# Retention with the last 16 keys as the left-over group, and other PSUM banks for the second feed-forward's first sums

## The chip, the cores and the metric

The kernel runs on one core of one Trainium2 chip. The metric is the device time of one execution in microseconds (us); less is better. Before the change it is 1469.22 us, the median of three runs (1469.2 to 1470.43).

## The reference

One block works on T = 528 tokens, 16 learned meta tokens followed by 512 real ones, of width 1024: a gated feed-forward, a mixer and a second gated feed-forward, each with a norm ahead and a residual sum behind it. The mixer projects its input to queries, keys, values and gates of two branches, retention and sparse attention, adds the two gated results and projects the sum. The part that matters here is retention, with 4 heads, keys of 256 and values of 512. The reference writes it chunk by chunk with a state:

```
inner = (q k^T * d_in) v            # within a chunk of 128 tokens
cross = (q state) * xi              # everything before the chunk
state = g_chunk * state + (k * zeta)^T v
y = concat(y_meta, inner + cross);  y = y / rms(y);  out = (silu(rg) * y) @ w_ret_out
```

Unrolled, the output of token i is the sum over all tokens j up to i of (q_i . k_j) times a power of the head's decay (the power is i - j) times v_j. The kernel computes it in that form. The meta tokens come first and every real token sees them. All numbers are fp32. The result holds the 512 real tokens.

## The kernel before

TensorE gets each fp32 operand as a high and a low part, and each product is three matmuls (high x high, high x low, low x high). The splits are a copy on ACT (the high part) and a subtraction on DVE or GpSimd (the low part), at lines 325 and 326 for most operands. Products go to PSUM. In the mixer four single banks (tag `sm`, taken in turn) and two double banks (tag `mm`) serve all products; a tile from a tag can be written once the tile that held that bank has been read.

The program is written out in one order (a manual schedule): each engine runs its instructions in the order in which the code issues them, and semaphores make it wait for others. The mixer is a list of steps, one for each tile of a projection's weights. Work of retention is hung into these steps.

For each head h:

- `fetch_head` and `new_decay` load values, gates and the table of decay powers from DRAM by SP's queue. `place_tails` (GpSimd's queue) puts the left-over values, the 16 meta tokens' in `vtail`, in three row groups (high, high, low).
- `values_in` (lines 1732 and 1735) splits the values.
- `decayed` (lines 1776 to 1800) makes five groups of score matmuls, six matmuls each. Groups `kb` = 0 to 3 hold 128 real keys, from token 16 + 128 kb on, against the 512 - 128 kb queries that can see them. The fifth holds the 16 meta keys against all 512 queries. Each product `psst` is multiplied by the decay on DVE into a scratch tile (`tmp`, four in turn) and split (`ph`, `pl`; `ptail` for the fifth).
- `weigh` (lines 1810 to 1821) multiplies the weights with the values, 128 queries at a time. One last matmul takes all left-over keys with its three products stacked in its rows (`ptail`, `vtail`). ACT squares the result for the norm, DVE multiplies it with the gate.

For head 0 this lies beside projections (`psgate`, `psrq`). For heads 1 to 3 it lies in `outputs(h-1)`, the four steps of the output projection of the head before. Each step makes two tiles `psro` in the `sm` banks, which ACT copies out (line 1955 into `accr`, or 1958 into `RR` for GpSimd to add). Behind the two tiles of step 1 come `values_in`, of step 2 `decayed`, of step 3 `weigh`. The gates' Silu (line 1745) is issued between the two tiles of step 2.

Values reach DRAM after their projection: the 512 real tokens' as `vrs`, the 16 meta tokens' by `last_tokens` (line 1400), which computes them in a small product behind the others and splits them, as `vd`.

The second feed-forward begins where the mixer's output tiles `psmo` end (line 158). `enter` (line 2690) closes the mixer's PSUM pools and opens `f2ps` for its first sums, `psd` (line 2653). The tags `d0` and `d1` come first in it. DVE adds each `psmo` tile to the residual (`hc`, line 2746).

Of the kernel before, what the change touches and what calls it, by code (L numbers as in the profile page):

```python
# [47 lines left out]

UW = NM + S


def _constants():

    pos = np.arange(T, dtype=np.float32)
    rope = np.zeros((3, 2, P, T), np.float32)
    for i, d in enumerate((64, 128, 256)):
        expo = -np.arange(0, d, 2, dtype=np.float32) / np.float32(d)
        freq = (10000.0 ** expo.astype(np.float64)).astype(np.float32)
        ang = (freq[:, None] * pos[None, :]).astype(np.float64)
        reps = P // (d // 2)  # L60
        cos = np.tile(np.cos(ang), (reps, 1))
        sin = np.tile(np.sin(ang), (reps, 1))
        if d < 256:
            sign = np.where((np.arange(P) % d) < d // 2, -1.0, 1.0)
            sin = sin * sign[:, None]
        rope[i, 0] = cos.astype(np.float32)
        rope[i, 1] = sin.astype(np.float32)
    decay = np.zeros((RH, P, UW), np.float32)
    diff = np.arange(UW)[None, :] - np.arange(P)[:, None]
    for h in range(RH):  # L70
        lg = math.log1p(-(2.0 ** (-5.0 - h)))
        decay[h] = np.where(diff >= 0, np.exp(lg * np.maximum(diff, 0)) * DK**-0.5, 0.0)
    causal = np.zeros((P, S), np.float32)
    p = np.arange(P)
    causal[:, S - P :] = np.where(p[None, :] <= p[:, None], 0.0, NEG)
    return {"rope": rope, "decay": decay, "causal": causal}
# [3 lines left out]
def kernel(ctx: ExitStack, tc: tile.TileContext, x, meta, g1, wg1, wu1, wd1, gm,  # L80
# [216 lines left out]
    vst = dpool.tile([2, P, 4, 4, P], F32, name="vst")  # L297
    vrs_d = dpool.tile([RH, P, 4, S], F32, name="vrs")
    rgs = dpool.tile([RH, 2, P, 2 * S], F32, name="rgs")
# [409 lines left out]
    if True:  # L709
# [574 lines left out]

        ret_k, ret_q = [], []
        tables = []

        def bring():
            hall_r = fp.tile([P, 4352], F32R, tag="hT", name="rqk")
            for at, c0, width, n in ((ret_k, 0, 576, T), (ret_q, 2304, S, S)):  # L1290
                off = width - n
                at.extend(tuple(hall_r[:, c0 + (2 * j + i) * width + off :][:, :n] for j in range(2)) for i in range(2))
            for i in range(2):
# [32 lines left out]
        class Values:  # L1326
# [36 lines left out]
            def leave(self, i, half, r):  # L1363
# [4 lines left out]
                elif self.kind == "values":  # L1368
                    nc.gpsimd.dma_start(vrs_d[i, :, 2 * half : 2 * half + 2, :].rearrange("p b c -> p (b c)"), r)
                else:  # L1370
                    nc.gpsimd.dma_start(rgs[i, half], r)
# [15 lines left out]
            def last_tokens(self):  # L1387
# [3 lines left out]
                for i, qs in enumerate((("11", "12"), ("21", "22"))):  # L1391
                    for k in range(KD):
                        for c in range(4):
                            nc.tensor.matmul(ps[32 * c : 32 * c + 32, i * P : (i + 1) * P], dv["last"][:, k, :],
                                             self.q[qs[k // 4]][:, k % 4, c * P : (c + 1) * P],
                                             start=k == 0, stop=k == KD - 1)
                r = room("rest")[:, : 4 * P]
                split(ps[:, : 2 * P], r[:, : 2 * P].bitcast(F32R), r[:, 2 * P :].bitcast(F32R))
                for i in range(2):
# [245 lines left out]
    if True:  # L1645
# [13 lines left out]
        def bring_more():  # L1659

            new_decay(0)
            fetch_head(0)
            place_tails(0)
            nc.gpsimd.dma_start(ka[:64, :S], fs[:64, 0, :])
# [40 lines left out]
        def new_decay(h):  # L1705
            u = heads[h]["u"] = rt.tile([P, UW], F32, tag="u", name="u")
            nc.sync.dma_start(u, decay[h])

# [3 lines left out]
        def fetch_head(h):  # L1712
# [3 lines left out]
            else:  # L1716
                v = vraw().rearrange("p (b c) -> p b c", b=4)
                vparts["l"] = [v[:, :2], v[:, 2:]]
            for i, v in enumerate(vparts["l"]):
                nc.sync.dma_start(v, vrs_d[h, :, 2 * i : 2 * i + 2])  # L1720
            heads[h]["g"] = [room4("g") for _ in range(2)]
# [6 lines left out]
        def values_in(h):  # L1728
# [4 lines left out]
            def low(i):  # L1733
                eng = nc.gpsimd if h else nc.vector
                eng.tensor_tensor(lo[i].bitcast(F32R), lo[i], hi[:, 2 * i : 2 * i + 2].bitcast(F32), ALU.subtract)
            low(0)
            if h:
                low(1)
            else:
                heads[0]["low"] = low  # L1740
# [35 lines left out]
        def decayed(h):  # L1776
            rq, rk, u = ret_q, ret_k, heads[h]["u"]
            prob, low = [], lambda: None
            for kb in range(5):
                kn, n, q0 = (P, S - kb * P, kb * P) if kb < 4 else (NM, S, 0)  # L1780
                ps = sm_tile("psst")
                ks = slice(NM + kb * P, NM + (kb + 1) * P) if kb < 4 else slice(0, NM)
                for k in range(2):
                    for i, (a, b) in enumerate(((rk[k][0], rq[k][0]), (rk[k][0], rq[k][1]), (rk[k][1], rq[k][0]))):
                        nc.tensor.matmul(ps[:kn, :n], a[:, ks], b[:, q0:],
                                         start=k == 0 and i == 0, stop=k == 1 and i == 2)
                t = tmp()
                u0 = 0 if kb < 4 else NM
                TT(t[:kn, :n], ps[:kn, :n], u[:kn, u0 : u0 + n], ALU.mult)
                low()  # L1790
                if kb < 4:
                    ph = rt.tile([P, n], F32R, tag=f"ph{kb}", name="ph")
                    pl = rt.tile([P, n], F32R, tag=f"pl{kb}", name="pl")
                    low = in_two(t[:, :n], ph, pl)
                    prob.append((ph, pl))
                else:
                    split_rows(t[:NM, :n], tp["p"], "hlh")
            heads[h]["prob"] = prob

        def weigh(h, b):  # L1800
# [5 lines left out]
            for kb in range(b + 1):  # L1806
                ph, pl = (p[:, (b - kb) * P : (b - kb + 1) * P] for p in d["prob"][kb])
                hi, lo = vh[:, kb, :], vl[kb // 2][:, kb % 2, :]
                for i, (a, v) in enumerate(((ph, hi), (ph, lo), (pl, hi))):
                    nc.tensor.matmul(ps, a, v, start=kb == 0 and i == 0, stop=False)  # L1810
            nc.tensor.matmul(ps, tp["p"][:TR, qs], tp["v"][:TR, :], start=False, stop=True)
            if b == 0:
                d["sum"] = rt.tile([P, 8], F32, tag="osum", name="osum", bufs=2)
            nc.scalar.activation(RR[:, 2 * S : 3 * S], ps, AF.Square, accum_out=d["sum"][:, b : b + 1])
            g = d["g"][b // 2][:, b % 2]
# [180 lines left out]
        def trip(h, between=None):  # L1996
# [4 lines left out]
            if h + 1 < RH:  # L2001
                place_tails(h + 1)

# [89 lines left out]
        tp.update(pool=rt, bufs=4)  # L2093
        tails(rt)
        ia, ib = (rt.tile([P, 4, S], F32, tag=f"o{c}", name="ixs") for c in "hl")
# [594 lines left out]
    def enter():  # L2690
# [4 lines left out]
        mixps.close()  # L2695
        f2["ps"] = ctx.enter_context(pool("f2ps", 1, PSUM))
        f2["rooms"] = ctx.enter_context(pool("rooms2", 1))
        f2["later"] = ExitStack()
# [357 lines left out]
```

## Time and profile before

| what | value |
|---|---|
| median of three runs | 1469.22 us (1469.2 to 1470.43) |
| the profiled execution, device time | 1468.84 us |
| its span, first to last instruction | 1467.1 us |
| TensorE busy | 1458.2 us, 99% of the span |
| VectorE (DVE) busy | 1151.5 us, 78% |
| ScalarE (ACT) busy | 781.4 us, 53% |
| GpSimd (POOL) busy | 288.8 us, 20% |
| mean granted TensorE clock | 0.999 |

The span is 1.7 us shorter than the device time of the same run. Busy shares are means over the whole span. An instruction's row in a timeline has its start, its duration, engine, line, operation, what it writes and reads with partitions x elements, how many like it follow each other (xN), and in brackets the idle time of its engine before it and what ended that. Durations of matmuls overlap: the distance of their starts tells what each costs.

### The profile page before, as it was taken

Reading aid. Unit: us, or ns where it says so; the run is one execution under the profiler, and the core shown is the slowest. Engines: PE = TensorE matmul, PEld = TensorE weight load, DVE = VectorE, ACT = ScalarE, POOL = GpSimd, SP = SyncE. Lnnn points to the kernel's source line nnn. Section 1 sums busy time; section 2 is a strip of 40 time slices with the busy share of each in tenths; the row PEclk is TensorE's granted clock in tenths of the full one; section 3 lists DMA queues with packets and bytes.
Section 4 is the critical chain, followed back from the end, with each engine's and each line's share of the span. In section 5 each row is a group of like instructions: output and inputs, shape, how many; then the busy total and the mean of one; then the engine's idle time right before and its main releaser. Section 6 shows DMA issues by size and latency. Waiting matters only on the chain.

```text
span 1467.1 us, 22451 instructions
## 1 busy us (share of the span) xinstructions
PE 1458.2 (99%) x8626; PEld 1286.1 (88%) x8626; DVE 1151.5 (78%) x1688; ACT 781.4 (53%) x1117; POOL 288.8 (20%) x354
## 2 busy tenths in 40 slices
PE   9999999999999999999999999999999999999998
PEld 8999999999988888888888889988888888888887
DVE  5998888876787986588788898888557787767776
ACT  6656455454354554567454547877534644434444
POOL 1101111002100001232152342444103211211110
PEclk9999999999999999999999999999999999999999
DMA  5458787556734554465336443676656476466323
GB/s 175 102 158 202 183 186 192 134 140 196 250 133 160 169 172 151 153 206 173 118 129 211 144 147 101 193 201 204 207 181 213 154 227 202 133 199 207 122 80 122
DMA packets 209563, 246.79 MB, mean 168 GB/s; under 512 B 31568, under 2 KB 153160, under 8 KB 209456
## 3 DMA queue, kind: packets, MB, share of 16 engines
q1 hardware_dynamic: 171504, 179.74, 38.6%
q0 software_dynamic: 34032, 58.78, 16.4%
q10 hardware_dynamic: 3920, 6.84, 1.4%
q8 instruction: 68, 1.11, 0.3%
q14 instruction: 39, 0.32, 0.1%
HBM read 205.52 MB, written 39.60 MB: 167 GB/s over the span
## 4 chain that ended last, share of the span: by engine, by line
PE 95%; DVE 2%; DMA 1%; ACT 1%; issue 0%; POOL 0%; ACTq 0%; DVEq 0%; POOLq 0%
PE psd L2781 8%; PE psvX L1431 7%; PE psqX L2616 7%; PE psqX L158 7%; PE psro L158 6%; PE psqZ L158 5%; PE psd L158 4%; PE psqY L2616 4%; PE psvY L1431 4%; PE psak L158 3%; PE psaq L158 3%; PE psga L158 3%; PE psat L158 3%; PE psmo L158 3%; PE psdX L158 2%; PE psrk L158 2%
## 5 line engine op out<-in xcount | busy, mean ns | idle before, releaser
L326 DVE TENSOR_TENSOR wlo<-raw,whi 128x1024 fp32r<-128x1024 f32 (+2 forms) x138 | 155.2, 1126 | 41.9 <-ACT whi L325 41.2
L325 ACT ACTIVATE whi<-raw 128x1024 fp32r<-128x1024 f32 (+2 forms) x138 | 130.0, 943 | 87.2 <-PE psat L158 9.4
L326 DVE TENSOR_TENSOR wlo<-w,whi 128x1024 fp32r<-128x1024 f32 x96 | 116.8, 1218 | 61.9 <-ACT whi L325 61.8
L325 ACT ACTIVATE whi<-w 128x1024 fp32r<-128x1024 f32 x96 | 101.6, 1058 | 103.7 <-PE psd L2781 39.3
L158 PE MATMUL psro<-o,whi 128*128 128x512 f32 x256 | 79.0, 390 | 0.0
L325 ACT ACTIVATE whi<-wsum 128x1024 fp32r<-128x1024 f32 (+1 forms) x48 | 48.3, 1006 | 36.9 <-PE psdY L158 10.3
L115 ACT ACTIVATE whi<-raw 128x1024 fp32r<-128x1024 f32 (+1 forms) x43 | 43.7, 1016 | 35.3 <-PE psat L158 12.2
L116 DVE TENSOR_TENSOR wlo<-raw,whi 128x1024 fp32r<-128x1024 f32 (+1 forms) x43 | 52.7, 1228 | 9.2 <-ACT whi L115 9.2
L2579 POOL DMA_DIRECT2D hts<-cross x40 | 26.0, 658 | 166.0 <-DVE cross L2576 166.0
L158 PEld LDWEIGHTS psro<-o,whi 128*128 128x128 f32 x256 | 47.9, 188 | 10.3
L2781 PE MATMUL psd<-wlo,hh 128*128 128x512 f32 (+1 forms) x148 | 56.7, 383 | 0.0
L2781 PE MATMUL psd<-whi,hl 128*128 128x512 f32 (+1 forms) x148 | 56.7, 383 | 0.0
L2781 PE MATMUL psd<-whi,hh 128*128 128x512 f32 (+1 forms) x148 | 56.7, 383 | 0.0
L326 DVE TENSOR_TENSOR wlo<-wsum,whi 128x1024 fp32r<-128x1024 f32 (+1 forms) x48 | 55.1, 1152 | 1.2 <-ACT whi L325 0.8
L1959 POOL TENSOR_TENSOR accr<-accr,RR 128x512 f32<-128x512 f32 x24 | 37.3, 1558 | 65.7 <-ACT RR L1958 65.7
L158 PE MATMUL psro<-o,wlo 128*128 128x512 f32 x128 | 49.8, 389 | 0.0
L1431 PE MATMUL psvX<-wlo,th 128*128 128x512 f32 x120 | 46.8, 390 | 0.0
L1431 PE MATMUL psvX<-whi,th 128*128 128x512 f32 x120 | 46.7, 389 | 0.0
L1431 PE MATMUL psvX<-whi,tl 128*128 128x512 f32 x120 | 46.7, 389 | 0.0
L158 PE MATMUL psqX<-xh,whi 128*128 128x264 f32 x144 | 40.8, 283 | 0.0
L158 PE MATMUL psqZ<-xh,wlo 128*128 128x264 f32 x144 | 40.8, 283 | 0.0
L158 PE MATMUL psqX<-xh,wlo 128*128 128x264 f32 x144 | 40.8, 283 | 0.0
(622 smaller groups left out, 5024.8 us busy)
## 6 DMA issues: line engine op xcount, KB each, us to landing
w<-in_w_in_dram SPq DMA_DIRECT2D x40, 512.0 KB, 4.6
raw<-in_w_in_dram SPq DMA_DIRECT2D x27, 512.0 KB, 4.2
raw<-in_w_in_dram SPq DMA_DIRECT2D x13, 1024.0 KB, 6.1
raw<-in_ffn_w_down_dram SPq DMA_DIRECT2D x24, 512.0 KB, 4.2
raw<-in_ffn_w_up_dram SPq DMA_DIRECT2D x11, 1024.0 KB, 5.1
raw<-in_ffn_w_gate_dram SPq DMA_DIRECT2D x10, 1024.0 KB, 5.2
ws<-in_ffn_w_up_dram POOLq DMA_DIRECT2D x20, 512.0 KB, 5.9
w<-in_ffn_w_up_dram SPq DMA_DIRECT2D x20, 512.0 KB, 5.0
```

The source lines that it names most:

```text
L115: nc.scalar.activation(hi, src, AF.Copy)
L116: eng.tensor_tensor(lo, src, hi.bitcast(F32), ALU.subtract)
L158: nc.tensor.matmul(o, a[:, k, :], b[:, sl], start=first and k == 0 and i == 0, stop=last and k == nk - 1 and i == 2, skip_group_check=onto)
L325: nc.scalar.activation(hi, src, AF.Copy)
L326: return lambda: nc.vector.tensor_tensor(lo, src, hi.bitcast(F32), ALU.subtract)
L1431: nc.tensor.matmul(d[bank_][t], a, b[:, k, :], start=not onto and j + k + m == 0, stop=j + k == 3 and m == 2, skip_group_check=onto)
L1959: nc.gpsimd.tensor_tensor(a, a, t, ALU.add)
L2579: nc.gpsimd.dma_start(d.rearrange("(b i) a e -> a i b e", i=32)[a], cross[32 * a : 32 * a + 32].rearrange("p b c t -> p b (c t)"))
L2616: nc.tensor.matmul(ps[:, t], a, b[:, k, :], start=not onto and j + k + m == 0, stop=j + k == 3 and m == 2, skip_group_check=onto)
L2781: nc.tensor.matmul(ps, a, m[:, j, cs], start=first and i == 0, stop=last and i == 2)
```

## The change

Tiles of keys now begin with the meta tokens: the four score groups hold tokens 0 to 127, 128 to 255 and so on of the 528. Queries stay cut at 16 + 128 b. The tile b of queries therefore sees the tiles of keys 0 to b, and what is left over for it are its own last 16 tokens as keys, which only the same 16 see as queries. The left-over keys of all four tiles are taken together in one group: 64 keys (4 x 16) against 64 queries (4 x 16), of which the four 16 x 16 blocks on the diagonal are used. The group has a decay table of its own, 64 x 64, with zeros off these blocks.

- The keys of the fifth group are not contiguous in SBUF; ACT copies them to a scratch tile in two copies (`last_k`, of 48 and 16 columns in four parts).
- `ptail` gets the diagonal blocks in 32-row pieces: four ACT copies and two DVE subtractions, each 32x2x16, instead of two and one of 16x512. The last matmul has 96 rows instead of 80.
- `vtail` holds the left-over values of two tiles side by side. `place_last` loads them unsplit by four DMAs of GpSimd's queue, and `split_last`, called in `values_in`, splits them by two ACT copies and one DVE subtraction of 32x1024. Before, split rows were loaded.
- The values are loaded by four DMAs instead of two, and the decay by two instead of one; `vrs` is laid out by rows of tokens. `last_tokens` copies the values by ACT without a split and sends half as many DMAs for them.
- The decay table takes the part of `RR` where the squares were written; the squares go to another part or to `caus`.
- In `enter`, two tiles with the tags `z` and `x` are taken first, so `d0` and `d1` lie in other banks.

```diff
-                    nc.gpsimd.dma_start(vrs_d[i, :, 2 * half : 2 * half + 2, :].rearrange("p b c -> p (b c)"), r)
+                    nc.gpsimd.dma_start(vrs_d[i, half * 2 * P : (half + 1) * 2 * P].rearrange("(b p) c -> p b c", p=P),
+                                        r.rearrange("p (b c) -> p b c", b=2))
...
+                if self.kind == "values":
+                    nc.scalar.activation(r[:, : 2 * P], ps[:, : 2 * P], AF.Copy)
+                    nc.gpsimd.dma_start(vd[2 * self.u : 2 * self.u + 2, 0].rearrange("i p d -> p i d"),
+                                        r[:, : 2 * P].rearrange("p (i d) -> p i d", i=2))
+                    return
...
+    TK = 3 * 2 * NM
+
+    def retention_tails(p):
+
+        t = p.tile([P, S], F32R, tag="ptail", name="ptail")
+        nc.gpsimd.memset(t[:TK].bitcast(F32), 0.0)
+        tp.update(v=p.tile([P, 2, S], F32R, tag="vtail", name="vtail"), p=t)
+
+    def place_last(h):
+
+        rows = vrs_d[h].rearrange("(b p) c -> b p c", p=P)
+        for b in range(4):
+            r = 4 * NM + b % 2 * NM
+            nc.gpsimd.dma_start(tp["v"][r : r + NM, b // 2].bitcast(F32), rows[b, P - NM :])
+
+    def split_last():
+
+        t, n = tp["v"], 2 * NM
+        for i in range(2):
+            nc.scalar.activation(t[i * n : (i + 1) * n], t[2 * n : 3 * n].bitcast(F32), AF.Copy)
+        return lambda: nc.vector.tensor_tensor(t[2 * n : 3 * n], t[2 * n : 3 * n].bitcast(F32), t[:n].bitcast(F32), ALU.subtract)
...
-            u = heads[h]["u"] = rt.tile([P, UW], F32, tag="u", name="u")
-            nc.sync.dma_start(u, decay[h])
+            u = heads[h]["u"] = RR[:, 2 * S : 3 * S], rt.tile([NT, NT + 16], F32, tag="ulast", name="ulast")[:, :NT]
+            nc.sync.dma_start(u[0], decay[h, :, NM:UW])
+            nc.sync.dma_start(u[1], decay[h, :NT, UW:])
...
-            for i, v in enumerate(vparts["l"]):
-                nc.sync.dma_start(v, vrs_d[h, :, 2 * i : 2 * i + 2])
+            a, b = vparts["l"]
+            rows = vrs_d[h, P - NM : S - NM].rearrange("(b p) c -> b p c", p=P)
+            nc.sync.dma_start(a[NM:, 0], vrs_d[h, : P - NM])
+            nc.sync.dma_start(a[:NM, 0].rearrange("q (c d) -> q c d", c=4), vd[h, 0].rearrange("(c q) d -> q c d", q=32)[:NM])
+            nc.sync.dma_start(a[:, 1], rows[0])
+            nc.sync.dma_start(b, rows[1:].rearrange("b p c -> p b c"))
...
+            last = split_last()
             low(0)
+            last()
...
-            for kb in range(5):
-                kn, n, q0 = (P, S - kb * P, kb * P) if kb < 4 else (NM, S, 0)
-                ps = sm_tile("psst")
-                ks = slice(NM + kb * P, NM + (kb + 1) * P) if kb < 4 else slice(0, NM)
+            def scored(ps, keys, queries):
                 for k in range(2):
-                    for i, (a, b) in enumerate(((rk[k][0], rq[k][0]), (rk[k][0], rq[k][1]), (rk[k][1], rq[k][0]))):
-                        nc.tensor.matmul(ps[:kn, :n], a[:, ks], b[:, q0:],
-                                         start=k == 0 and i == 0, stop=k == 1 and i == 2)
-                t = tmp()
-                u0 = 0 if kb < 4 else NM
-                TT(t[:kn, :n], ps[:kn, :n], u[:kn, u0 : u0 + n], ALU.mult)
+                    for i, (a, b) in enumerate(((0, 0), (0, 1), (1, 0))):
+                        nc.tensor.matmul(ps, keys[k][a], queries(rq[k][b]), start=k == 0 and i == 0, stop=k == 1 and i == 2)
+
+            last_k = tmp().bitcast(F32R)[:, : 4 * NT].rearrange("p (a b q) -> p a b q", a=4, q=NM)
+            for do, of in zip((last_k[:, :, :3], last_k[:, :, 3]), last_of):
+                nc.scalar.activation(do, of.bitcast(F32), AF.Copy)
+            for kb in range(4):
+                n = S - kb * P
+                ps = sm_tile("psst")[:, :n]
+                scored(ps, [[t[:, kb * P : (kb + 1) * P] for t in rk[k]] for k in range(2)], lambda t: t[:, kb * P :])
+                t = tmp()[:, :n]
+                TT(t, ps, u[0][:, :n], ALU.mult)
                 low()
-                if kb < 4:
-                    ph = rt.tile([P, n], F32R, tag=f"ph{kb}", name="ph")
-                    pl = rt.tile([P, n], F32R, tag=f"pl{kb}", name="pl")
-                    low = in_two(t[:, :n], ph, pl)
-                    prob.append((ph, pl))
-                else:
-                    split_rows(t[:NM, :n], tp["p"], "hlh")
+                ph = rt.tile([P, n], F32R, tag=f"ph{kb}", name="ph")
+                pl = rt.tile([P, n], F32R, tag=f"pl{kb}", name="pl")
+                low = in_two(t, ph, pl)
+                prob.append((ph, pl))
+            ps = sm_tile("psst")[:NT, :NT]
+            scored(ps.rearrange("p (b q) -> p b q", q=NM), [[last_k[:, 2 * j + i].rearrange("p b q -> p (b q)") for j in range(2)] for i in range(2)], lambda t: t.rearrange("p (b q) -> p b q", q=P)[:, :, P - NM :])
+            t = tmp()[:NT, :NT]
+            TT(t, ps, u[1], ALU.mult)
+            low()
+            last = tp["p"].rearrange("p (a b q) -> p a b q", a=2, q=P)
+            for a in range(2):
+                at = slice(a * 2 * NM, (a + 1) * 2 * NM)
+                src = t[at, at].rearrange("p (b q) -> p b q", q=NM)
+                h_, l_, again = (last[i * 2 * NM : (i + 1) * 2 * NM, a, :, P - NM :] for i in range(3))
+                nc.scalar.activation(h_, src, AF.Copy)
+                nc.scalar.activation(again, src, AF.Copy)
+                TT(l_, src, h_.bitcast(F32), ALU.subtract)
...
-            nc.tensor.matmul(ps, tp["p"][:TR, qs], tp["v"][:TR, :], start=False, stop=True)
+            nc.tensor.matmul(ps, tp["p"][:TK, qs], tp["v"][:TK, b // 2], start=False, stop=True)
...
-            nc.scalar.activation(RR[:, 2 * S : 3 * S], ps, AF.Square, accum_out=d["sum"][:, b : b + 1])
+            nc.scalar.activation(caus if h else RR[:, :S], ps, AF.Square, accum_out=d["sum"][:, b : b + 1])
...
+        for t in "zx":
+            f2["ps"].tile([P, 1024], F32, tag=t, name="later")
```

On ACT, head 1: from the value copies (`vh`) over the gates (`g`) to the eviction of the last output tile before the scores (`accr5` from `psro`) and the first split of scores (`ph`). Before:

```order
L1732 ACTIVATE vh_7302<-vraw_7207 128x1024 [waits DMAHW7_49]
L1732 ACTIVATE vh_7302<-vraw_7207 128x1024 [waits DMAHW0_49]
L325 ACTIVATE whi_7309<-raw_7187 128x1024 [waits DMAHW6_49]
L1955 ACTIVATE accr4_7200<-psro_7312 128x512 [waits PE_49]
L1745 ACT_TABLE_LOAD
L1745 ACTIVATE g_7210<-g_7210 128x1024 [waits DMAHW1_49]
L1745 ACTIVATE g_7211<-g_7211 128x1024 [waits DMAHW2_49,DMASW7_49,DMASW0_49]
L1955 ACTIVATE accr5_7201<-psro_7329 128x512 [waits PE_49]
L325 ACTIVATE ph_7352<-tmp_7350 128x512 [waits DVE_49]
```

and after:

```order
L1772 ACTIVATE vh_7314<-vraw_7216 128x1024 [waits DMAHW4_49,DMAHW3_49,DMAHW2_49]
L1772 ACTIVATE vh_7314<-vraw_7216 128x1024 [waits DMAHW5_49]
L1635 ACTIVATE vtail_6534<-vtail_6534 32x1024 [waits DMASW5_49,DMASW6_49,DMASW4_49,DMASW3_49]
L1635 ACTIVATE vtail_6534<-vtail_6534 32x1024
L329 ACTIVATE whi_7324<-raw_7196 128x1024 [waits DMAHW1_49]
L2010 ACTIVATE accr4_7209<-psro_7327 128x512 [waits PE_49]
L1787 ACT_TABLE_LOAD
L1787 ACTIVATE g_7221<-g_7221 128x1024 [waits DMAHW6_49]
L1787 ACTIVATE g_7222<-g_7222 128x1024 [waits DMAHW7_49,DMASW7_49,DMASW0_49]
L2010 ACTIVATE accr5_7210<-psro_7344 128x512 [waits PE_49]
L1828 ACTIVATE tmp_7358<-rqk_5207 128x4x48 [waits DVE_49]
L1828 ACTIVATE tmp_7358<-rqk_5207 128x4x16
```

Two copies into `vtail` now stand behind the value copies, and two copies into `tmp` (the last keys) behind the eviction.

On TensorE, head 1: the third, fourth and fifth score group and the first matmul of the next output tile. Before:

```order
L1785 MATMUL psst_7368<-rqk_5209 128x256 [waits Activation_49]
L1785 MATMUL psst_7368<-rqk_5209 128x256 x5
L1785 MATMUL psst_7381<-rqk_5209 128x128 [waits DVE_49]
L1785 MATMUL psst_7381<-rqk_5209 128x128 x5
L1785 MATMUL psst_7394<-rqk_5209 16x512 [waits DVE_49]
L1785 MATMUL psst_7394<-rqk_5209 16x512 x5
L158 MATMUL psro_7410<-o_7006,whi_7261 128x512 [waits Activation_49]
```

and after:

```order
L1824 MATMUL psst_7386<-rqk_5207 128x256 [waits Activation_49]
L1824 MATMUL psst_7386<-rqk_5207 128x256 x5
L1824 MATMUL psst_7399<-rqk_5207 128x128 [waits Activation_49]
L1824 MATMUL psst_7399<-rqk_5207 128x128 x5
L1824 MATMUL psst_7412<-rqk_5207,tmp_7358 64x64 [waits DVE_49,Activation_49]
L1824 MATMUL psst_7412<-rqk_5207,tmp_7358 64x64 x5
L162 MATMUL psro_7431<-o_7015,whi_7273 128x512 [waits DVE_49]
```

The fourth group waited for DVE and now waits for ACT: its bank is the one that `accr5_7210<-psro_7344` empties. The fifth waits for DVE and for ACT's copies into `tmp_7358`, and the output tile behind it for DVE instead of ACT.

On TensorE, the passage from the mixer's last output tile to the second feed-forward's first sums. Before:

```order
L158 MATMUL psmo_11639<-ml_11297,whi_11557 128x512
L158 MATMUL psmo_11639<-mh_11296,wlo_11558 128x512
L2653 MATMUL psd_11705<-whi_11598,xh0_11364 128x512 [waits DVE_49,Activation_49]
L2653 MATMUL psd_11705<-whi_11598,xl0_11365 128x512
L2653 MATMUL psd_11705<-wlo_11599,xh0_11364 128x512
```

and after:

```order
L162 MATMUL psmo_11686<-ml_11344,whi_11604 128x512
L162 MATMUL psmo_11686<-mh_11343,wlo_11605 128x512
L2708 MATMUL psd_11754<-whi_11645,xh0_11411 128x512 [waits Activation_49]
L2708 MATMUL psd_11754<-whi_11645,xl0_11412 128x512
L2708 MATMUL psd_11754<-wlo_11646,xh0_11411 128x512 [waits DVE_49]
```

The wait for DVE moves from the first matmul, which begins the bank, to the third, which reads the low part of the weights (`wlo`).

## Rows read from the trace of the kernel before

**Rows 1.** The page, part 1: each engine's busy time, share of the span, instructions.
```profile
PE 1458.2 (99%) x8626; PEld 1286.1 (88%) x8626; DVE 1151.5 (78%) x1688; ACT 781.4 (53%) x1117; POOL 288.8 (20%) x354
```

**Rows 2.** Waits of TensorE: us in total, times, longest us.
```profile
PE psd L2653 <- DVE hc L2746: 0.9, 1, 0.9
```

**Rows 3.** Groups of TensorE by form, 691.5 to 697.2 us: busy us, mean ns.
```profile
L1785 PE MATMUL psst<-rqk 128*16 128x512 f32 x6 | 1.6, 396 | 0.0
L1785 PE MATMUL psst<-rqk 128*128 128x128 f32 x6 | 0.8, 266 | 0.0
```

**Rows 4.** Timeline of TensorE, heads 0 to 3: start us, us, work, idle before it.
```profile
619.52 5.32 PE L1785 MATMUL psst<-rqk 128*128 128x512 f32 x30
624.67 0.40 PE L158 MATMUL psrq<-xh,whi 128*128 128x512 f32 x1
...
691.72 5.32 PE L1785 MATMUL psst<-rqk 128*128 128x512 f32 x30
696.87 0.63 PE L158 MATMUL psro<-o,whi 128*128 128x512 f32 x2
...
754.16 0.63 PE L158 MATMUL psro<-o,whi 128*128 128x512 f32 x2
...
811.46 0.63 PE L158 MATMUL psro<-o,whi 128*128 128x512 f32 x2
```

**Rows 5.** Timeline of ACT, head 1, from the value copies on.
```profile
688.67 2.00 ACT L1732 ACTIVATE vh<-vraw 128x1024 fp32r<-128x1024 f32 x2
690.57 1.05 ACT L325 ACTIVATE whi<-raw 128x1024 fp32r<-128x1024 f32 x1
691.52 0.58 ACT L1955 ACTIVATE accr<-psro 128x512 f32<-128x512 f32 x1
692.12 1.28 ACT L1745 ACT_TABLE_LOAD   x1
693.41 2.01 ACT L1745 ACTIVATE g<-g 128x1024 f32<-128x1024 f32 x2
695.32 0.58 ACT L1955 ACTIVATE accr<-psro 128x512 f32<-128x512 f32 x1
695.80 1.03 ACT L325 ACTIVATE ph<-tmp 128x512 fp32r<-128x512 f32 x2
...
697.51 0.42 ACT L325 ACTIVATE ph<-tmp 128x256 fp32r<-128x256 f32 x1 [0.68 <-DVE tmp L1789]
698.18 0.31 ACT L325 ACTIVATE ph<-tmp 128x128 fp32r<-128x128 f32 x1 [0.25 <-DVE tmp L1789]
```

**Rows 6.** Timeline of ACT, heads 2 and 3: the eviction after the gates.
```profile
751.32 0.60 ACT L1958 ACTIVATE RR<-psro 128x512 f32<-128x512 f32 x1
...
808.44 0.59 ACT L1958 ACTIVATE RR<-psro 128x512 f32<-128x512 f32 x1
```

**Rows 7.** Timeline of ACT, DVE and SP's queue, head 0.
```profile
619.24 1.06 ACT L1732 ACTIVATE vh<-vl 128x1024 fp32r<-128x1024 f32 x1 [1.41 <-DMA vl<-vrs]
620.21 0.58 ACT L1904 ACTIVATE RR<-psgate 128x512 f32<-128x512 f32 x1
...
621.08 0.69 DVE L1789 TENSOR_TENSOR tmp<-psst,u 128x512 f32<-128x512 f32 x1 [1.99 <-PE psst L1785]
...
628.65 1.22 DVE L1735 TENSOR_TENSOR vl<-vl,vh 128x1024 fp32r<-128x1024 f32 x1
...
609.32 1.00 SPq L1720 DMA_DIRECT2D vl<-vrs  x2
```

**Rows 8.** Timeline of all engines where the second feed-forward's first sums begin.
```profile
1127.49 0.39 PE L158 MATMUL psmo<-ml,whi 128*128 128x512 f32 x1
...
1127.72 0.39 PE L158 MATMUL psmo<-mh,wlo 128*128 128x512 f32 x1
1128.14 0.69 DVE L2746 TENSOR_TENSOR hc<-psmo,hc 128x512 f32<-128x512 f32 x1 [0.33 <-PE psmo L158]
...
1128.98 0.47 PE L2653 MATMUL psd<-whi,xh 128*128 128x512 f32 x1 [0.88 <-DVE hc L2746]
```

More of the change, by code (lines that the diff above doesn't have):

```diff
@@ L49 @@
 UW = NM + S
+NT = 4 * NM
 def _constants():
@@ L67, in _constants @@
         rope[i, 1] = sin.astype(np.float32)
-    decay = np.zeros((RH, P, UW), np.float32)
+    decay = np.zeros((RH, P, UW + NT), np.float32)
     diff = np.arange(UW)[None, :] - np.arange(P)[:, None]
@@ L71, in _constants @@
         lg = math.log1p(-(2.0 ** (-5.0 - h)))
-        decay[h] = np.where(diff >= 0, np.exp(lg * np.maximum(diff, 0)) * DK**-0.5, 0.0)
+        decay[h, :, :UW] = np.where(diff >= 0, np.exp(lg * np.maximum(diff, 0)) * DK**-0.5, 0.0)
+        for b in range(4):
+            at = slice(b * NM, (b + 1) * NM)
+            decay[h, at, UW + b * NM : UW + (b + 1) * NM] = decay[h, :NM, :NM]
     causal = np.zeros((P, S), np.float32)
@@ L297 @@
     vst = dpool.tile([2, P, 4, 4, P], F32, name="vst")
-    vrs_d = dpool.tile([RH, P, 4, S], F32, name="vrs")
+    vrs_d = dpool.tile([RH, S, S], F32, name="vrs")
     rgs = dpool.tile([RH, 2, P, 2 * S], F32, name="rgs")
@@ L1283 @@
         beside = [beside_0, lambda: next(dv["norm"]), beside_2, beside_3, beside_4, beside_5, beside_6, beside_7, beside_8]
-        ret_k, ret_q = [], []
+        ret_k, ret_q, last_of = [], [], []
         tables = []
@@ L1292, in bring @@
                 at.extend(tuple(hall_r[:, c0 + (2 * j + i) * width + off :][:, :n] for j in range(2)) for i in range(2))
+            parts = hall_r[:, : 4 * 576].rearrange("p (a t) -> p a t", a=4)[:, :, 48 + P :]
+            last_of.append(parts[:, :, : 3 * P].rearrange("p a (b q) -> p a b q", q=P)[:, :, :, :NM])
+            last_of.append(parts[:, :, 3 * P :])
             for i in range(2):
@@ L1601, in tails @@
         tp.update(v=stacked(p, "vtail", S), p=stacked(p, "ptail", S))
+    TK = 3 * 2 * NM
[5 more added lines that the diff above has]
+        rows = vrs_d[h].rearrange("(b p) c -> b p c", p=P)
+        for b in range(4):
+            r = 4 * NM + b % 2 * NM
[5 more added lines that the diff above has]
+        return lambda: nc.vector.tensor_tensor(t[2 * n : 3 * n], t[2 * n : 3 * n].bitcast(F32), t[:n].bitcast(F32), ALU.subtract)
     def values_of(parts):
@@ L1662, in bring_more @@
             fetch_head(0)
-            place_tails(0)
+            place_last(0)
             nc.gpsimd.dma_start(ka[:64, :S], fs[:64, 0, :])
@@ L2001, in trip @@
             if h + 1 < RH:
-                place_tails(h + 1)
+                place_last(h + 1)
         def arrived(h, halves=(0, 1)):
@@ L2093 @@
         tp.update(pool=rt, bufs=4)
-        tails(rt)
+        retention_tails(rt)
         ia, ib = (rt.tile([P, 4, S], F32, tag=f"o{c}", name="ixs") for c in "hl")
```

## Prediction

> **What bounds the kernel now.** I read the page first: TensorE is busy for 1458.2 of 1467.1 us [rows 1], so the time is TensorE's own stream plus what little it waits, and an edit counts only by what it adds to or takes from that stream. Then the waits of TensorE: the one they show near the edited code is 0.9 us at the start of the second feed-forward [rows 2]. TensorE does not wait at all in the score groups of retention, the other place of the change. So no stall is there to be removed in retention; columns can be, and a wait can appear. Then the timeline of TensorE and of ACT, row by row, around these places.
>
> TensorE issues a matmul of 512 columns every 0.23 us (1127.49 to 1127.72) [rows 8]. The six matmuls of the 16 meta keys move 512 columns each and occupy TensorE like those of 128 keys [rows 3], so they cost 6 x 0.23 = 1.38 us. All thirty score matmuls of a head take 5.15 us (619.52 to 624.67, and 691.72 to 696.87) [rows 4]. Take off 12 x 0.23 for the 512-column ones and, by columns, 6 x 0.17 and 6 x 0.115 for those of 384 and 256; 0.68 is left for the six of 128 columns, 0.11 each.
>
> **The change, part by part.**
>
> *The fifth score group: 6 matmuls of 16 x 512 become 6 of 64 x 64.* No matmul of 64 columns by 64 keys is in the trace. Bounds: 0.11 us each (as at 128 columns) and 0.03 (64/512 of 0.23). I take 0.06, half of the 128-column one. Each head then saves 6 x 0.17 = 1.0 us of TensorE (0.7 to 1.2), the four heads 4.0 (2.9 to 4.8), if nothing waits. [...]
>
> *ACT in heads 1 to 3.* Before the scores ACT splits the values in two copies of 128x1024, which start 0.95 us apart and take 1.05 (2.00 for two) [rows 5]. The change adds two copies of 32x1024 behind them. Fewer partitions do not make an ACT copy cheaper by the rows at hand, since time goes with elements per partition (0.58 at 512, 1.05 at 1024) [rows 5], so I take 2 x 0.95 = 1.9 us; nothing is the lower bound. These copies stand in front of the two evictions of retention's output tiles (accr<-psro). Before, the second of these (695.32 to 695.90 in head 1) released only the psro tile after the scores, which starts at 696.87, so it had 1 us to spare. The order shows that now the fourth score group waits for ACT, where it waited for DVE: it takes the bank that this eviction empties. It would start at about 691.72 + 6 x (0.23 + 0.17 + 0.115) = 694.8 if nothing waited. From the first value copy at 688.67 to the eviction ACT has no idle time (each row begins as the former ends, the table load of 1.28 among them) [rows 5]. So 1.9 us more in front moves the eviction by 1.9.
> Head 1: the eviction ends at 695.90 + 1.9 = 697.80; TensorE goes on some 0.15 later (as from the end of hc, 1128.83, to psd at 1128.98) [rows 8]; the fourth group takes 6 x 0.11, the fifth 6 x 0.06, and the next psro starts at 699.0, against 696.87 [rows 4]: **+2.1 us**.
> Head 2: eviction 751.32 + 0.60 + 1.9 = 753.82 [rows 6], next psro at about 755.0 against 754.16 [rows 4]: **+0.8**.
> Head 3: 808.44 + 0.59 + 1.9 = 810.93 [rows 6], next psro at 812.1 against 811.46 [rows 4]: **+0.65**. Heads 2 and 3 lose less as they have no table load there.
> The fifth group waits besides for two new ACT copies of the last keys (192 and 64 elements; between 0.31 for 128 and 0.42 for 256 [rows 5], so I take 0.36 and 0.3, started together some 0.5 after the eviction does). They run beside the fourth group; without that cover they would cost 0.5 us a head. Bounds for the three heads together: -3.0 (nothing waits) to +5.0 (that cover gone).
> This place rests on ACT not letting the eviction pass the copies in front of it. [...]
>
> *Head 0.* There the second value copy waits for its load and starts at 619.24, the gate's eviction follows at 620.21 [rows 7]. After it: two copies at 620.2 and 621.15, the eviction 622.1 to 622.7, the key copies to about 623.3. DVE gets the subtraction of the 32 rows ahead of the first score product: from 622.2 for 1.22 us (as another 1024 elements took) to 623.4, then the first product, 0.69 [rows 7], to 624.1. The fifth group waits for that product (624.2 to 624.6); the second product takes the scratch buffer that the last keys held until then and ends at about 625.3; the next projection tile waits for it: 625.4 against 624.67, **+0.8**. The value loads are now four and the decay two, so three more SP issues stand before the last value load; two of them took 1.00 us [rows 7], so up to 1.5 us more: +2.3 is the upper bound, -1.0 (no wait) the lower.
>
> *Second feed-forward.* The last psmo and the first psd start 1.26 us apart, two psmo 0.23 [rows 8]. In between psd waits for DVE, which empties psmo (hc, 1128.14 to 1128.83): the first sums lie in the bank psmo used. The order shows that the wait for DVE moves off the first psd matmul; what is left is ACT's weight split, long done. **-1.0 us**. What is late next is the low weight half for the third matmul, also done by then. Bounds: -1.0 to 0 (the microsecond is lost at the next tile, whose input must also arrive).
>
> *At nothing:* the 96-row instead of 80-row tail matmul (same columns); the smaller ptail copies and the two subtractions fewer on DVE at the values, which run beside a TensorE that does not wait for them; the larger number of DMAs on POOL, whose cover is the whole output stage of the head before.
>
> Sum: 0.8 + 2.1 + 0.8 + 0.65 - 1.0 = +3.3 us. The profiled run took 1468.84, so 1472.15; the median of the runs shown is 0.38 above that run, so **1472.5** is forecast for the median.
>
> **Rivals.**
> *A, faster:* the new waits don't bind, as when ACT gets through its copies earlier than I think or the fourth group's wait is for something long done. For it: TensorE's own work does become shorter in every head. Against it: the closed row of ACT work [rows 5]. It gives -4.0 - 1.0 = -5.0, about 1464.2. It decides as soon as the eviction ends before 694.7 in head 1.
> *B, no difference:* ACT's copies of 32 rows are cheaper or hide (say 1 us per head rather than 1.9), so that head 1 costs 1.2, heads 2 and 3 about nothing, head 0 nothing, and the feed-forward gives its microsecond: +0.2, about 1469.5.
> *C, slower still:* the value loads of head 0 land late (+1.5 on top), and the feed-forward gives nothing (+1.0): +5.8, about 1475. For it: both loads of head 0 were waited for already, the second for as long as 1.4 us before 619.24 [rows 7].
>
> **How the numbers follow.** Forecast 0.45 (its own range 1471 to 1474), A 0.2, B 0.2, C 0.15. A change of under 0.2% (2.9 us) can't be told from none here, so slower begins at 1472.2 and faster ends at 1466.3. Slower: C and 0.27 of the forecast's 0.45, 0.42. Same: the rest of the forecast, B but for 0.02, about 0.36. Faster: A and that rest of B, 0.22. The range leaves out half of A at the bottom and a part of C at the top: 1464.5 to 1475.5.
>
> **What would show it.** In the waits of TensorE after: psst waiting for ACT's accr or RR copies, longest in head 1 (about 3 us before the fourth group) and about 1.5 to 2 in heads 2 and 3; two ACT rows of 32x1024 of about 1.05 us; psd without a wait for hc, 0.23 after psmo. In TensorE's timeline thirty psst rows in about 7.3 us in head 1 instead of 5.15. Wrong if psst shows no wait, if the 32x1024 copies take half, or if a matmul of 64 columns takes over 0.11 us.

## The result and the profile after

The changed kernel takes 1487.59 us (median of 4 runs, 1483.84 to 1490.8), the kernel before 1469.21. The ratio is 1.0123, 95% interval 1.0098 to 1.0148: slower by 18 us, where 3.3 were forecast. The profiled run is the shortest, 1483.84 us, with a span of 1481.8 and a mean granted clock of 0.995. The page, part 1:

```profile
PE 1462.2 (99%) x8626; PEld 1290.3 (87%) x8626; DVE 1153.4 (78%) x1694; ACT 791.5 (53%) x1141; POOL 286.7 (19%) x355
```

TensorE is busy 4 us longer than before [rows 1], although its instructions are the same in number and move fewer columns in sum. Its waits (us in all, times, longest) have five new lines, all in the score groups or right behind them, 11.7 us together:

```profile
PE psst L1824 <- DVE tmp L1834: 3.1, 3, 1.3
PE psst L1824 <- ACT RR L2013: 3.1, 3, 1.4
PE psst L1824 <- ACT accr L2010: 2.8, 1, 2.8
PE psst L1824 <- ACT RR L1959: 2.0, 1, 2.0
...
PE psrq L162 <- DVE tmp L1834: 0.7, 1, 0.7
```

The line of psd and hc [rows 2] is gone. The timeline of TensorE in heads 0, 1 and 2 (start, us, work, idle before; head 3 has the same two waits as head 2, 1.40 and 1.29 us):

```profile
618.80 3.28 PE L1824 MATMUL psst<-rqk 128*128 128x512 f32 x18
624.06 0.89 PE L1824 MATMUL psst<-rqk 128*128 128x128 f32 x6 [1.99 <-ACT RR L1959]
625.51 0.51 PE L1824 MATMUL psst<-rqk,tmp 128*64 128x64 f32 x6 [0.56 <-DVE tmp L1834]
626.74 0.62 PE L162 MATMUL psrq<-xh,whi 128*128 128x512 f32 x1 [0.72 <-DVE tmp L1834]
...
695.12 3.55 PE L1824 MATMUL psst<-rqk 128*128 128x512 f32 x18
701.50 1.05 PE L1824 MATMUL psst<-rqk 128*128 128x128 f32 x6 [2.83 <-ACT accr L2010]
702.35 0.79 PE L1824 MATMUL psst<-rqk,tmp 128*64 128x64 f32 x6
702.95 1.20 PE L162 MATMUL psro<-o,whi 128*128 128x512 f32 x2
...
756.34 2.58 PE L1824 MATMUL psst<-rqk 128*128 128x512 f32 x12
759.18 0.97 PE L1824 MATMUL psst<-rqk 128*128 128x256 f32 x6 [0.27 <-ACT RR L2013]
761.56 0.89 PE L1824 MATMUL psst<-rqk 128*128 128x128 f32 x6 [1.41 <-ACT RR L2013]
763.73 0.82 PE L1824 MATMUL psst<-rqk,tmp 128*64 128x64 f32 x6 [1.28 <-DVE tmp L1834]
764.36 1.20 PE L162 MATMUL psro<-o,whi 128*128 128x512 f32 x2
```

Against [rows 4], head 1 began its scores at 695.12 instead of 691.72, and reached the next psro after 7.8 us instead of 5.15 (heads 0, 2 and 3 took 7.9, 8.0 and 7.9 us to the tile behind their scores, 5.15 each before). The fourth group (128x128) waits in every head, and in heads 0, 2 and 3 the fifth (64 columns) as well. The first score matmul of head 0 starts 0.7 us earlier than before, those of heads 1 to 3 start 3.4, 7.3 and 11.5 us later and the last psmo 15.7 later, so each head costs 3.9 to 4.2 us. The order of ACT in head 1, beside [rows 5]:

```profile
691.92 2.00 ACT L1772 ACTIVATE vh<-vraw 128x1024 fp32r<-128x1024 f32 x2
693.94 2.13 ACT L1635 ACTIVATE vtail<-vtail 32x1024 fp32r<-32x1024 f32 x2
...
698.95 2.00 ACT L1787 ACTIVATE g<-g 128x1024 f32<-128x1024 f32 x2
700.86 0.58 ACT L2010 ACTIVATE accr<-psro 128x512 f32<-128x512 f32 x1
```

The eviction (accr at 700.86) starts 8.94 us after the first value copy; before it was 6.65. So two copies of 32x1024 cost 2.3 us, not 1.9, and the fourth group starts 0.06 after the eviction ends. DVE in head 2, in a second fence GpSimd beside it, and in a third the subtraction in all four heads (ns, min/median/max, then first and last start):

```profile
757.59 3.17 DVE L1636 TENSOR_TENSOR vtail<-vtail 32x1024 fp32r<-32x1024 f32 x1 [2.43 <-ACT vtail L1635]
760.97 2.01 DVE L330 TENSOR_TENSOR wlo<-raw,whi 128x1024 fp32r<-128x1024 f32 x1 [0.20 <-DVE vtail L1636]
762.91 1.14 DVE L1834 TENSOR_TENSOR tmp<-psst,RR 128x512 f32<-128x512 f32 x2
```

```profile
754.88 4.80 POOL L1775 TENSOR_TENSOR vraw<-vraw,vh 128x1024 fp32r<-128x1024 f32 x2
```

```profile
L1636 DVE TENSOR_TENSOR vtail<-vtail x4: 1217/3006/3187, 623.4 to 818.9; 32x1024 fp32r<-32x1024 f32 x4
```

In head 0, where GpSimd has no such work, the subtraction of 32x1024 takes 1.22 us, as a subtraction of this length does in [rows 7]; here it takes 3.17. GpSimd's two subtractions of the values run from 754.88 to 759.68; DVE's ends 1.1 us after that, at 760.76. Behind it stands the subtraction for the weights (wlo), which was there before too, and so the first score product, which frees the bank of the fifth group, only comes at 762.91. In head 0 (ACT) the second value copy starts a microsecond later than in [rows 7], as its load lands later, and the eviction 3.2 us later:

```profile
620.19 1.06 ACT L1772 ACTIVATE vh<-vl 128x1024 fp32r<-128x1024 f32 x1 [2.23 <-DMA vl<-vrs]
...
623.41 0.60 ACT L1959 ACTIVATE RR<-psgate 128x512 f32<-128x512 f32 x1
```

At last the granted clock behind these waits (windows; the columns are in the first line, PEclk is the clock):

```profile
core 0: us, PE busy (x) PEld busy (x) DVE busy (x) ACT busy (x) POOL busy (x), PEclk, DMA share, GB/s
626.00:632.00 6.00, 5.28 (x17) 4.22 (x17) 5.26 (x11) 2.77 (x9) 2.57 (x6) 0.72 1.04 355
702.00:706.00 4.00, 4.00 (x18) 3.43 (x18) 2.72 (x9) 2.83 (x9) 0.00 (x0) 0.57 0.00 0
762.00:767.00 5.00, 3.72 (x17) 3.09 (x16) 4.59 (x11) 2.25 (x7) 2.11 (x1) 0.66 0.02 3
823.00:829.00 6.00, 4.71 (x21) 3.92 (x22) 5.07 (x12) 3.10 (x11) 2.41 (x2) 0.72 0.56 174
```

PEclk is a mean over the window. Each stretch has a part that reads 0.50 (627 to 630, 703 to 705, 764 to 766, 825 to 828), and no window of 1 us in them reads less; in the kernel before, all windows of 5 us from 600 to 850 read 1.00. The four windows lack 6 x 0.28, 4 x 0.43, 5 x 0.34 and 6 x 0.28 us, each time 1.7 us of full speed: 6.8 us in all. It is seen in the matmuls too: the two psro at 702.95 take 1.20 us, those at the same place before 0.63 [rows 4].

And the start of the second feed-forward, as in [rows 8]:

```profile
1143.39 0.39 PE L162 MATMUL psmo<-mh,wlo 128*128 128x512 f32 x1
1143.62 0.39 PE L2708 MATMUL psd<-whi,xh 128*128 128x512 f32 x1
```

0.23 us between them instead of 1.26. The account: waits +11.7, clock +6.8, shorter fifth groups -4, feed-forward -1.0, makes +13.5; the two spans differ by 14.7. The other 1.2 us are about what the nine waits cost beside their idle time, by an estimate: a matmul of 512 columns lasts 0.39 us and the next starts 0.23 us after it, and a wait loses this overlap of 0.16 us each time.

### The profile page after: what moved, and what is told of

The parts are those of the page before. It is cut to its first block, busy times and chain, and to the rows that moved or that the text cites. A ratio compares the mean times of both kernels' runs of the same rounds, so it can differ in the third digit from the quotient of the medians.

```text
span 1481.8 us, 22540 instructions
## 1 busy us (share of the span) xinstructions
PE 1462.2 (99%) x8626; PEld 1290.3 (87%) x8626; DVE 1153.4 (78%) x1694; ACT 791.5 (53%) x1141; POOL 286.7 (19%) x355
## 4 chain that ended last, share of the span: by engine, by line
PE 90%; DVE 5%; ACT 2%; issue 1%; DMA 1%; POOL 0%; DVEq 0%; ACTq 0%; SPq 0%; POOLq 0%
PE psd L2838 8%; PE psqX L2671 7%; PE psvX L1444 7%; PE psqX L162 7%; PE psqZ L162 5%; PE psd L162 4%; PE psqY L2671 4%; PE psvY L1444 4%; PE psak L162 3%; PE psaq L162 3%; PE psga L162 3%; PE psat L162 3%; PE psmo L162 3%; PE psro L162 3%; PE psdX L162 2%; PE psrq L162 2%
## 5 line engine op out<-in xcount | busy, mean ns | idle before, releaser
L162 PE MATMUL psro<-o,whi 128*128 128x512 f32 x256 | 82.0, 402 | 0.0
L162 PE MATMUL psqX<-th,wlo 128*128 128x264 f32 x144 | 40.7, 283 | 0.0
```

What stands on the lines that cost most here:

```text
L162: nc.tensor.matmul(o, a[:, k, :], b[:, sl], start=first and k == 0 and i == 0, stop=last and k == nk - 1 and i == 2, skip_group_check=onto)
```

## The experiments

Theory after this reading: three causes in a row. ACT's two copies stand in front of the eviction that frees the fourth group's bank; DVE's subtraction stands in front of the product that frees the fifth's; and the pauses lower the clock. Rivals: the matmuls of 64 columns lower the clock; or ACT's copies alone explain all.

**psum_only**: of the change only the last hunk of the diff, on the kernel before.

> Only the edit of the PSUM tags of the second feed-forward, on the kernel before. Theory (the edit does what the traces show of it): the first psd follows the last psmo by 0.23 us instead of 1.26, nothing else moves, 0.9 to 1.0 us less than before, ratio about 0.9994. Rival (the microsecond is lost again later in the feed-forward): the same time as before.

Measured 1468.85 us, ratio 0.9988 (0.9977 to 0.9998). The first psd follows at 1128.54, 0.23 behind the psmo at 1128.31. The gain stays to the end of the run: from that psmo to the end of the span it is 338.3 us, before 339.4. So the theory holds, and this part of the change is good for the microsecond that was forecast. (The interval alone, 0.3 to 3.4 us, would not tell its size.)

**sub_late**: DVE's subtraction behind the score groups.

```diff
-            last()
...
+            heads[h]["last"]()      # at the end of decayed
```

> The changed kernel with DVE's subtraction of the left-over values issued at the end of the score groups, ACT's two copies where they were. Theory: the fifth group's wait for DVE goes (1.3 us in heads 2 and 3, 0.6 in head 0, where the wait of the tile behind it, 0.7, goes as well), the fourth group's wait for ACT stays (1.4 to 2.8 us), and the half clock after it stays; about 4 us less than the changed kernel, 1483 to 1485. Rival (the ACT copies alone make all of it, DVE comes late only because it waits for them): no gain.

Measured 1480.45 us, ratio 1.0068 (1.005 to 1.0086), 7 us less than the changed kernel, more than expected. The profiled runs differ by less, 3.0 us, as the changed kernel's is its shortest. No line for the fifth group is left, and those for ACT are as they were in heads 1 to 3. The wait of psrq in head 0 (0.7) stays, against the expectation. The clock in heads 2 and 3:

```profile
762.00:768.00 6.00, 4.60 (x29) 3.85 (x28) 4.96 (x12) 4.30 (x13) 3.17 (x2) 1.00 0.01 3
820.00:827.00 7.00, 5.60 (x35) 4.71 (x34) 5.92 (x13) 5.29 (x14) 3.50 (x3) 1.00 0.47 150
```

In both heads the fourth group still waits 1.4 us, but with the second wait gone the clock stays at 1.00. That is the part beyond the expectation. Behind the waits of heads 0 and 1 it still falls (0.57 in the 8 us from 626, 0.72 in the 6 us from 704), in head 0 for longer than in the changed kernel; the mean granted clock of this run is 0.996.

**gates_late**: the Silu copies behind the groups, the subtraction where the change has it.

```diff
                             decayed(h + 1)
+                            open_gates(h + 1)
...
-                if i == 2:
-                    open_gates(h + 1)
```

> The changed kernel with the gates' Silu (two ACT copies of 1024 and in head 1 the table load) issued behind the score groups, so that the eviction before them is no longer behind them; the copies and the subtraction of the left-over values stay. Theory (ACT's copies and DVE's subtraction are two causes side by side): the fourth group's wait for ACT goes, but the first score product on DVE still comes 3 us late, so the fifth group waits for it, some 2 us in head 1 and 3 in heads 2 and 3; the time hardly falls, 1483 to 1487. Rival (ACT alone): no wait in heads 1 to 3, about 1473.

Measured 1484.89 us, ratio 1.0103 (1.0086 to 1.012). The wait went from ACT to DVE, as expected, and the rival (ACT alone) fails; the 2.2 us for ACT in the second line are at the third group of heads 2 and 3:

```profile
PE psst L1824 <- DVE tmp L1834: 7.4, 4, 2.9
PE psst L1824 <- ACT RR L2013: 2.2, 2, 2.0
```

**gates_and_sub_late**: both, and in head 0 ACT's copies between the splits.

> Both causes taken away in heads 1 to 3: the Silu behind the score groups and DVE's subtraction of the left-over values behind them too. In head 0 ACT's two copies stand between the splits of the scores instead of in front of the gate's eviction. Theory: no wait of psst in heads 1 to 3 and no fall of the clock, every head 1 us shorter but head 0, 1465 to 1467, better than before. Rival (what is moved back is late at the weights times values): waits of pspv for vtail or for the gates, 1469 to 1472.

Measured 1474.83 us, ratio 1.0034 (1.0019 to 1.0048). The expectation of a gain was wrong. Small waits of psst stayed (1.9 us for DVE in three heads, 0.9 for ACT), and in head 2 two of them, 0.5 and 0.7 us, were followed by a stretch at a lower clock (0.76 in the 7 us from 756, 1.7 us of full speed). In head 3 waits of 0.4 and 0.7 us at the same two groups were not (the mean granted clock of the run, 0.998, leaves room for one such stretch beside the 0.999 of the kernel before).

**split_late**: ACT's copies and DVE's subtraction behind the score groups.

```diff
-            last = split_last()
             low(0)
-            last()
...
+            split_last()()          # at the end of decayed
```

> The changed kernel with both, ACT's two copies and DVE's subtraction of the left-over values, issued at the end of the score groups. Theory (the pauses come from these three instructions in front of the evictions, and the half clock from the pauses): no wait in heads 2 and 3, 1 us in head 1, nearly none in head 0; granted clock back at 1.0 in heads 2 and 3 although the 64x64 matmuls are there; 1465 to 1468. Rival (the 64-column matmuls, not the pauses, pull the clock down): it still falls in all four heads for some 5 us, and the time is 1470 or more.

Measured 1476.96 us, ratio 1.0042 (1.003 to 1.0054): the score groups are as the theory has them, the total is not. The last matmul of the weights times values now waits for vtail:

```profile
PE pspv L1865 <- DVE vtail L1636: 3.9, 2, 2.0
```

In head 0 the same matmul starts 1.4 us late besides. In head 2 the six matmuls of 64 columns and the next psro, without a pause before them (first fence, TensorE), and the clock over the groups of heads 1 to 3 (second, columns as above):

```profile
757.59 0.48 PE L1822 MATMUL psst<-rqk,tmp 128*64 128x64 f32 x6
757.91 0.70 PE L162 MATMUL psro<-o,whi 128*128 128x512 f32 x2
```

```profile
700.00:706.00 6.00, 5.69 (x33) 4.90 (x34) 2.72 (x9) 4.84 (x13) 0.00 (x0) 1.00 0.00 0
756.00:762.00 6.00, 6.00 (x39) 5.31 (x38) 5.36 (x9) 2.88 (x9) 5.44 (x3) 1.00 0.01 3
816.00:822.00 6.00, 6.00 (x39) 5.32 (x38) 5.39 (x9) 2.87 (x9) 5.39 (x3) 1.00 0.55 175
```

0.32 us for six: 0.053 each, and the clock is full with 64-column matmuls in all three heads. So the rival (64 columns lower the clock) fails. The clock drops only later, behind the wait of pspv in head 2 (2.0 us), among matmuls of 512 columns; behind that in head 3 (1.9 us) it does not:

```profile
764.00:772.00 8.00, 5.99 (x20) 4.54 (x19) 5.17 (x8) 4.30 (x8) 4.97 (x5) 0.79 0.04 8
824.00:832.00 8.00, 6.09 (x27) 4.72 (x26) 5.35 (x9) 5.47 (x12) 4.04 (x3) 1.00 0.01 2
```

**pause_in_before**: the kernel before, with ACT delayed and nothing of the change in it.

```diff
-                nc.scalar.activation(hi[:, 2 * i : 2 * i + 2], lo[i], AF.Copy)
+                for _ in range(3 if h else 1):
+                    nc.scalar.activation(hi[:, 2 * i : 2 * i + 2], lo[i], AF.Copy)
```

> The kernel before with the two value copies of heads 1 to 3 issued three times over (four more ACT copies of 128x1024 a head, 3.8 us), all else as before. Theory: the output tile behind the score groups waits for its bank, 2.9 us in head 1, 1.5 in head 2, 1.4 in head 3, and the clock falls to half for some us behind each, as in the changed kernel: 5.8 us of waiting and about 3.6 from the clock, 1478 to 1479. Rival (64-column matmuls pull the clock down): waits alone, clock 1.0 all through, about 1475.

Measured 1491.16 us, ratio 1.0137 (1.0116 to 1.0158). It waits earlier than expected, at the third and the fourth group, 12 us in all; TensorE in head 1 and, second, the windows behind the waits:

```profile
698.47 0.98 PE L1786 MATMUL psst<-rqk 128*128 128x256 f32 x6 [2.06 <-ACT accr L1956]
701.17 4.10 PE L1786 MATMUL psst<-rqk 128*128 128x128 f32 x12 [1.72 <-DVE tmp L1790]
```

```profile
704.00:710.00 6.00, 6.00 (x20) 4.42 (x19) 3.93 (x8) 3.47 (x6) 0.00 (x0) 0.70 0.00 0
768.00:774.00 6.00, 6.00 (x19) 3.98 (x17) 3.90 (x9) 3.04 (x5) 0.00 (x0) 0.62 0.00 0
832.00:838.00 6.00, 6.00 (x18) 3.78 (x18) 3.93 (x8) 3.04 (x5) 0.50 (x1) 0.55 0.43 151
```

The clock falls in all three heads without a 64-column matmul; these windows lack 6.8 us of full speed. The size expected was well short (9 us over the kernel before, and 21 were measured: twice the waiting, and more from the clock), but the direction is clear: the pauses do it.

**gpsimd_late** (GpSimd's subtraction issued later) told nothing apart: GpSimd has nothing else to do between, so it began when it did before, and DVE's subtraction in head 2 took 3.17 us again (1486.69 us, one run).

> The changed kernel with GpSimd's subtraction of the values in heads 1 to 3 issued behind the score groups. It tells why DVE's subtraction of 32x1024 takes 2.8 to 3.2 us in heads 1 to 3 and 1.2 in head 0. Theory (it runs beside GpSimd's subtraction): 1.2 to 1.3 us in all heads, the first score product about 2 us sooner, the fifth group's wait for it gone, the fourth group's for ACT as it was. Rival (32 partitions with sources in three row groups make it slow, or it waits in itself): 2.8 to 3.2 us again. Weights times values then wait for GpSimd, so the total says nothing.

**low_on_dve**: what GpSimd subtracts in heads 1 to 3 is left to DVE, behind the groups.

> The changed kernel with the low halves of the values in heads 1 to 3 made by DVE behind the score groups instead of by GpSimd in front of them (in gpsimd_late GpSimd had nothing else in its queue and began at the same time as before, so nothing was told apart). Theory (DVE's subtraction of 32x1024 is slow where GpSimd's subtraction runs beside it): 1.2 to 1.3 us in head 1, where GpSimd now has nothing to do, instead of 2.8, and nearer 1.2 than 3.2 in heads 2 and 3, where GpSimd only adds to the accumulators. Rival (it is slow by its own operands): 2.8 to 3.2 us again.

One run, 1483.61 us. DVE's subtractions of vtail in the four heads (ns, min/median/max):

```profile
L1636 DVE TENSOR_TENSOR vtail<-vtail x4: 1216/1217/1218, 628.1 to 821.8; 32x1024 fp32r<-32x1024 f32 x4
```

1.22 us in all four, and the fifth group's wait for DVE in heads 2 and 3 goes with it; the clock then stays at 1.00 in these two heads, as in sub_late. So GpSimd's subtraction beside it made the 3 us. (The total tells little: it is one run, and DVE has GpSimd's work on top.) In the changed kernel DVE's instruction ends 1.1 us after GpSimd's second one in heads 1, 2 and 3, about its own plain length, whether it began 1.75 us before that end (head 1: 2.84 us in all) or 2.1 (heads 2 and 3: 3.17 and 3.19). By an estimate from these times, it gained next to nothing from the part that lay beside GpSimd's; what holds it up was not shown.

**copies_between**: ACT's copies behind the first and second split (`ph`), the subtraction at the end.

```diff
+                if kb < 2:
+                    heads[h]["copy"](kb)
...
+            heads[h]["last"]()
```

> As sub_late, but ACT's two copies of the left-over values stand between the splits of the scores in all heads; the Silu stays where it was. Theory: ACT is as before up to the eviction, so psst waits 1.0 us in head 1 alone, the clock holds, and weights times values find vtail ready or wait less than the 2 us of split_late; 1466 to 1470. Rival: the two copies delay the later splits and the wait of split_late only changes its name, 1472 to 1476.

Measured 1469.33 us, ratio 0.9995 (0.9985 to 1.0005). Waits, and the clock around them:

```profile
PE psst L1827 <- ACT RR L2019: 1.4, 1, 1.4
PE psst L1827 <- ACT accr L2016: 1.0, 1, 1.0
```

```profile
696.00:704.00 8.00, 6.98 (x38) 5.99 (x39) 4.15 (x11) 7.40 (x16) 0.67 (x1) 1.00 0.00 0
810.00:818.00 8.00, 6.73 (x37) 5.78 (x38) 6.21 (x13) 6.93 (x15) 5.92 (x3) 1.00 0.43 131
```

Pauses of 1.0 and 1.4 us here are not followed by a fall. Against the kernel before the loss is gone, but so is the gain: the waits that are left cost about what the shorter groups and the PSUM edit save.

**gates_and_copies_between** and **mixed** tried to get below the kernel before:

> The two before together: Silu and subtraction behind the score groups, the copies between the splits, in all heads. Theory: no psst wait at all; ACT has the most work behind the groups here, so a wait of pspv for the gates or for vtail is the risk; 1465 to 1470. Rival: that work behind the groups costs more than the 1 us a head that the score groups save, 1470 to 1474.

> The copies between the splits and the subtraction behind them in all heads, as in copies_between; of the gates' two Silu in head 1 both, in head 3 one stand behind the score groups, in head 2 none. Theory: no wait of psst in head 1 (1.0 in copies_between), under half a microsecond in head 3 (1.4), and no wait for the gates behind; 1 to 2 us less than copies_between, 1467 to 1468.5, ratio 0.998 to 0.999. Rival (what the order gains here is lost at the weights times values): as copies_between, 0.9995.

The first took 1471.08 us, ratio 1.0009 (0.9999 to 1.002), the second 1469.0, ratio 0.9992 (0.9983 to 1.0001). In mixed the psst waits are nearly gone (0.4 us), but the weights times values wait for the gates (0.7), and head 0 keeps its wait for the scratch buffer that the last keys hold (psrq, 0.7).

No order tried makes the retention part pay; the version to keep is psum_only.

## Why the prediction was wrong

The direction was right, and so was one step: ACT's two copies move the eviction, and the fourth group waits for it. The size was not: +3.3 us, 1464.5 to 1475.5, against +18. From the first score matmul to the tile behind the scores heads 0 to 3 took 2.8, 2.7, 2.9 and 2.7 us more than before, where +0.8, +2.1, +0.8 and +0.65 were forecast; behind that tile the slow clock brings each to the 3.9 to 4.2 above.

- *Clock, the term that is missing.* The step "the fourth group takes 6 x 0.11, the fifth 6 x 0.06, and the next psro starts at 699.0" counts TensorE at full speed behind a pause. It was not: 1.7 us a head in the profiled run, 6.8 of the 14.7. The trace of before has nothing above 1.1 us among its waits of TensorE and no fall behind them (all windows of 10 us from 0 to 1460 read 1.00; only the end, 1464 to 1467, where TensorE has no more matmuls, reads 0.50), so the price could not be read there; but the prediction forecast a wait of 3 us and did not ask what it would do. The repeats of the changed kernel were 3 to 7 us longer still, at mean clocks of 0.991 to 0.993, so the profiled run is its mildest.
- *DVE's subtraction.* It was priced at 1.22 us and in head 0 alone; in heads 1 to 3 it was put at nothing without a reason. There it takes 2.8 to 3.2, behind GpSimd's subtraction. The +0.8 and +0.65 of heads 2 and 3 left it out: there it added the fifth group's wait of 1.3 us, and with it the fall of the clock. The two heads cost 4.1 and 4.2. sub_late, which takes only this away, gives back 7 us.
- *ACT's copies.* 2.3 us instead of 1.9; the forecast start of the fourth group in head 1 (3.15 us late) was nearly met, 3.3. ACT's rows started in the order of the program (691.92 to 701.34 in head 1), as this step takes for granted. It held; with the eviction where it was (copies_between), the longest of these waits falls to 1.4 us.
- *Head 0.* The late value load and the row of waits were in the bounds (up to +2.3), but not in the sum (+0.8). With the clock it came to 4.
- *The 64-column matmul* was taken at 0.06 us and measured 0.053. *The feed-forward's microsecond* was right.

What DVE pays beside GpSimd stood in the trace of before. In head 2, while GpSimd's subtractions of the values ran (747.58 to 753.36), a DVE subtraction of 128x1024 took 2.00 us, against 1.22 in [rows 7]:

```profile
749.08 2.00 DVE L326 TENSOR_TENSOR wlo<-raw,whi 128x1024 fp32r<-128x1024 f32 x1 [1.23 <-ACT whi L325]
```

Rival A fails as the prediction said it would. Rival C named late loads in head 0, and it was the nearest.

## What to carry to other kernels

A pause of the engine that sets the time has a price of its own: before a wait is put into TensorE's stream, price it twice, as time and as the clock behind it (1.7 us a head in the changed kernel, nothing behind the single pauses of 1.0 and 1.4 in copies_between), and count close waits together. When instructions are added in front of an eviction, look at who takes the emptied bank next, since the pool may give it to an earlier user than before. A subtraction on DVE beside a subtraction on GpSimd is to be priced with about what is left of the other's running instruction on top (here 2.84 and 3.17 us instead of 1.22, with 1.75 and 2.1 us left).

## What was not expected of the hardware

- Single pauses of 1.0, 1.4 (copies_between) and 1.9 us (split_late, head 3) left the clock at 1.0. Single pauses of 2.0 us (split_late, head 2) and 2.8 us (changed kernel, head 1), and three of 0.27, 1.41 and 1.28 close together (changed kernel, head 2), were each followed by a stretch at a lower clock (0.79 over 8 us, 0.57 over 4, 0.66 over 5) that cost 1.7 us. So were two of 0.5 and 0.7 us in head 2 of gates_and_sub_late, but not two of 0.4 and 0.7 in its head 3. What decides in between stays open.
- DVE's subtraction of 32x1024 took 3.17 us where it began beside GpSimd's (changed kernel, head 2) and 1.22 without it (low_on_dve); it ended 1.1 us after GpSimd's.
